# Two more split stages at the start of a fast-matrix-product kernel, earlier and smaller weight casts, and 2 KB pieces in DRAM

## The chip, the cores and the metric

The kernel runs on one core of a Trainium2 chip. The metric is the device time of one execution in microseconds (us). Three executions of the kernel before took 1366.88 to 1367.45 us, their median is 1367.18.

## The reference

`x` is 8192 rows (16 x 512) of 512 numbers. Each row has 8 router logits; a softmax makes 8 probabilities of them. There are 8 expert matrices of 512 x 2048. The output is the sum over the experts of probability times product:

```python
probs = softmax(router_logits)
for e in range(8):
    output += probs[:, :, e:e+1] * np.matmul(x, expert_weights[e])
```

Put otherwise, it is one product: a left matrix of 8192 rows and 8 x 512 columns (each row of x times each of its probabilities) times the stacked experts, 4096 rows and 2048 columns.

## The kernel before

**The recursion.** The big product isn't computed by the plain rule, but by a form of fast matrix multiplication in which a 2 x 2 block product takes 7 block products in place of 8, at the price of sums of blocks on both sides. This is done on two levels everywhere and on a third level in some places. The outer level makes products of the kinds r = 1 to 7 (code: `product(r, q)`, q = 0 to 15 names a pair of row blocks of 256). Product 1, called P1, multiplies the upper half of the experts (block B11, experts 0 to 3, columns 0 to 1023) and needs no sums of weights. The weights' blocks are B11, B12, B21 and B22, each in quarters (k, n) of 1024 x 512. Operands are float16, sums in PSUM are float32.

**Products, steps, stages, slots.** On the second level each product has seven steps in the order 1, 5, 6, 2, 7, 3, 4 (`STEPS`, L344), each of 8 matmuls with 512 columns, for output quarters of 128 x 512. Two products a and b make a stage. A stage has 14 slots, in which the steps take turns: slot 0 is step 1 of a, slot 1 step 1 of b, slot 2 step 5 of a, and so on (`run`, L875). Stages 0 to 5 hold P1 for q = 2, 3 and on to 12, 13. A step accumulates in one of three PSUM banks of its product, x (steps 1, 6, 7, 4), q (5, 3) and b (2). After a step, `post` (L551) copies or adds: in P1, steps 7 and 3 are an addition on VectorE (DVE) into an `h` tile ("accumulation" in what follows), the rest copies on ScalarE (ACT).

**Left operands.** For each product DVE makes `z` (t[0] and t[1], x times probability, 128x2048 float16), a difference `d` (s2, 128x1024) and "i" (z minus d). Step 1 and 5 need t[0], step 6 needs d, 2 and 4 need t[1], 7 and 3 need i. On the right, steps 5, 6, 7 and 4 need sums of weight quarters (`inner_sums`, L169), which are also made on DVE: "sum 5" to "sum 4", 128x4096 each.

**Split stages.** In a split stage (`third`, L823; `run_third`, L856) the steps 1 and 5 of both products, 32 matmuls, are themselves done by 7 products instead of 8. They are 14 parts, x1 to x7 (for step 1) and q1 to q7 (for step 5), of 4 matmuls with 256 columns each. They need four sums `s` of the two left operands (`Third.make`, L633) and four sums `t` of each of the two right operands (`Split.make`, L606), all 128x1024. After x5 and q5 ACT copies two halves of a bank (L661, L663); after x6, q6, x7 and q7 DVE adds (L666). So that PE doesn't wait for these, two pieces of other work are held back and put between the parts (`held`): the last two slots of the stage before (steps 4 of a and b). The order is x1 x5 q1 q5, held piece, x2 q2 x6 q6, held piece, x7 q7 x3 q3 x4 q4, then slots 4 to 13. Before the change P1's stages 2 to 5 are split (L1219), further stage 9 and six stages near the end.

**The order of DVE's work.** DVE executes in the order in which the code emits. The code keeps a queue of tasks (`later`, L370) and two clocks, "pe" and "dve" (L348). Each slot adds SLOT = 1.73 to pe; then, while dve is more than LAG = 0.3 behind pe, the next task is emitted and its cost added to dve (`slack`, L375; costs 1.14 for a z or i, 0.61 for d, s and t, 2.2 for a sum of weights). An accumulation is emitted after that, and adds 0.61 (`evacuated`, L381). A part of a split stage adds 0.44 to pe and emits no task; what it needs and what isn't there yet is emitted at once (`need`, L365). The left operands of stage k + 1 are queued at slot 1 of stage k (`queue_lefts`, L828): for a split stage both t[0], four `s`, both d, both t[1].

**Queues of transfers.** GpSimd (POOL) issues the stores of results and all casts of weights from float32 (`cast_w`, L145, 512 KB each), in the order of the code; SyncE (SP) issues loads of probabilities pT and x blocks, and transposes; ACT issues the fetches of kept weights and operands from DRAM (`fetch_w`, L164; `Operand.fetch`, L513). `at(stage, slot, ...)` (L698) puts something ahead of a slot. Weight tiles come from a pool of 15 buffers, `z` from 8, `h` from 13, x and pT from 9.

**Wedges.** From stage 4 to 9 (`wedge_at`, L982) a half of a quarter of B12 and of B22 is cast into one tile, 1024 KB in two casts, at slot 2; at slot 11 three DVE tasks are queued that make u = b - a, then two more sums in place, each stored to DRAM by POOL.

**The first phase** (L308 to L340) computes the plain product for the first rows (q = 0 and 1): it makes `z0` by small matmuls, then for two column halves n = 0, 1 runs e = 0 to 3 with 16 matmuls each, with the four results of a half copied by ACT (L337) and stored by SP. In between are the softmax and the first transposes `xT` and probabilities `pT` for stage 0. The end of the phase queues stage 0's work (L1234 to L1245).

Of the kernel before, what the change touches and what calls it, by code (L numbers as in the profile page):

```python
# [31 lines left out]
def kernel(  # L32
# [7 lines left out]
    nc = tc.nc  # L40
# [202 lines left out]
    def diag_e(e):  # L243
        return diag(ph0[0][:, e].unsqueeze(2))
# [15 lines left out]
    def early_xp1(j, d):  # L260
# [7 lines left out]
        evacuate(xp1[t][1][:, :, rows], ps.rearrange("p (e t) -> p e t", e=HE), 1)  # L268

    R = 4  # L270
    J = HQ // R
# [43 lines left out]
    for e in (1, 2):  # L315
        ds_.append(diag_e(e + 1))
        early_z0(e, ds_[e])
    for n in range(2):
        ps = [bank() for _ in range(4)]
        for e in range(HE):  # L320
            if n == 0 and e == 1:
                early_z0(3, ds_[3])
                ph0.append(early_p(1))
                ds_ = [diag_j(j) for j in range(4, 8)]
                keep_p = softmax_of_all()
                w, sums = inner_sums(b11, new_w())
# [8 lines left out]
        for j in range(4):  # L335
            o = half()
            act(nc.scalar.copy(o, ps[j]))  # L337
            sp(kept[j // 2][n].rearrange("(p j) m -> j p m", j=2)[j % 2], o)
        if n == 0:
            keep_p()  # L340

# [94 lines left out]
    class Left:  # L436
# [38 lines left out]
        def store(self, k):  # L475
            sp(self.kept[:, k], self.t[k])

# [29 lines left out]
    class Operand:  # L507
# [5 lines left out]
        def fetch(self):  # L513
            self.t = wpool.tile([P, 2, K8, HQ], f16, name="o", tag="w")
            note(nc.scalar.dma_start(out=self.t, in_=self.source))

# [75 lines left out]
    THIRD = (1, 5)  # L592
    COLS = [ds(i * HQ, HQ) for i in range(2)]

    class Split:
# [10 lines left out]
        def make(self, p, i):  # L606
            if i == 0:
                self.t[p] = wpool.tile([P, 4, C, HQ], f16, name="t", tag="w")
            w, t = self.right.op(p), self.t[p]
            block = lambda k, n: w[:, ds(k * C, C), COLS[n]]  # L610
            x, y = ((block(0, 1), block(0, 0)), (block(1, 1), t[:, 0]), (block(1, 1), block(0, 1)),
                    (block(1, 0), t[:, 1]))[i]
            tt(t[:, i], x, y, SUB)

        def op(self, p, m):
            if m in (1, 2, 3):
                k, n = ((0, 0), (1, 0), (1, 1))[m - 1]
                return self.right.op(p)[:, ds(k * C, C), COLS[n]]
            i = {5: 0, 6: 1, 7: 2, 4: 3}[m]
            need(self.task[p, i])  # L620
            return self.t[p][:, i]
# [125 lines left out]
    def product(r, q, **how):  # L747
# [18 lines left out]
        elif r == 6:  # L766
# [188 lines left out]
    def wedge(kn, e):  # L955

        t = new_w()
        a, b = t[:, ds(0, C), :], t[:, ds(C, C), :]
        rows = ds(e * C, C)

        def casts():
            cast_w(12, kn, e, a)
            cast_w(22, kn, e, b)

        def send(what, u):
            pool(kept_w(what, kn)[:, rows, :], u)

# [14 lines left out]
    def wedge_at(stage, slot, kn, e, then):  # L982
        made = []

        def begin():
            casts, made_ = wedge(kn, e)
            casts()
            made.extend(made_)

        def go_on():  # L990
            for make in made:
                later(1.14, make)
        at(stage, slot, begin)
        at(*then, go_on)

    b21, t1, t2, t3 = {}, {}, {}, {}

    def cast21(kn):
        b21[kn] = cast_block(21, kn)

    for i, kn in enumerate(((0, 0), (0, 1), (1, 1), (1, 0))):
        at(i + 1, 2, lambda kn=kn: cast21(kn))

# [25 lines left out]
    def odd_t():  # L1029
# [5 lines left out]
        def make3():  # L1035
            tt(made[12], made[22], made[12], SUB)
            pool(kept_w("t3", ODD), made.pop(12))

# [6 lines left out]
    def odd_t4():  # L1045
        def make():
            tt(made[21], made[21], t2[ODD], SUB)
            pool(kept_w("t4", ODD), made.pop(21))
        later(2.2, make)
# [34 lines left out]

    def part_of(what, kn, chunks):
        return kept_w(what, kn)[:, chunks, :]

    last_part = [None]

    def by_parts(stage, slot, every, r, load, between, when):  # L1090

        for j in range(4):
# [8 lines left out]

            def go_on(b=b, chunks=chunks):
                for kn in b:
                    if kn != ODD:
                        between(b[kn], kn, chunks)

            def end(b=b, chunks=chunks):
                last_part[0] = sums_in_place(lambda p, o: pool(part_of((r, p), (0, 0), chunks), o), b, r, 0.61, r == 3)
            at(*slots_after(stage, slot, j * every), begin)
# [11 lines left out]
    def load_part(what):  # L1121
        def load(t, kn, j, chunks):
            pool(t, part_of(what, kn, chunks))
        return load
# [3 lines left out]

    def less_t2(t, kn, chunks):
        def make():  # L1130
            tt(t, t, t2[kn][:, chunks, :], SUB)
            pool(part_of("t4", kn, chunks), t)
        later(0.61, make)

    def keep_raw(t, kn, chunks):
        pool(part_of("b22", kn, chunks), t)

# [138 lines left out]
```

## Time and profile before

| | us |
|---|---|
| median of 3 executions | 1367.18 |
| profiled execution | 1367.07 |
| its span (first to last instruction) | 1365.1 |
| PE busy | 1359.9 |
| DVE busy | 1126.5 |
| POOL busy | 407.0 |
| ACT busy | 195.7 |

A row of a timeline has the start (us from the span's start), the duration, the engine, the line, the operation, output<-inputs, the shape and the number of instructions merged into it, and in brackets the idle time before it and who ended that. Where instructions follow closely, a duration of 0.69 overlaps the next, which starts 0.6 later. A row of waits has who waited for whom, the total, how often, and the longest. The row on landing gives the least, middle and largest time from a transfer's issue to its arrival. A row of a DMA queue has its packets, megabytes, and the share of 16 engines' span that its packets took; a row of DMA issues has the count, the size and the middle time to landing.

### The profile page before, as it was taken

Reading aid. Unit: us, or ns where it says so; the run is one execution under the profiler, and the core shown is the slowest. Engines: PE = TensorE matmul, PEld = TensorE weight load, DVE = VectorE, ACT = ScalarE, POOL = GpSimd, SP = SyncE. Lnnn points to the kernel's source line nnn. Section 1 sums busy time; section 2 is a strip of 40 time slices with the busy share of each in tenths; the row PEclk is TensorE's granted clock in tenths of the full one; section 3 lists DMA queues with packets and bytes.
Section 4 is the critical chain, followed back from the end, with each engine's and each line's share of the span. In section 5 each row is a group of like instructions: output and inputs, shape, how many; then the busy total and the mean of one; then the engine's idle time right before and its main releaser. Section 6 shows DMA issues by size and latency. Waiting matters only on the chain.

```text
span 1365.1 us, 18194 instructions
## 1 busy us (share of the span) xinstructions
PE 1359.9 (100%) x6657; PEld 648.7 (48%) x6657; DVE 1126.5 (83%) x1367; ACT 195.7 (14%) x362; POOL 407.0 (30%) x644
## 2 busy tenths in 40 slices
PE   9999999999999999999999999999999999999998
PEld 4455544544444444444444444444444444456554
DVE  5975787989789788788887888888889797998873
ACT  3232311100011111111111100000000000123221
POOL 3123333331223342333322122242332422223232
PEclk9999999999999999999999999999999999999999
DMA  9999999999898999999999978989898979999896
GB/s 195 242 218 228 253 242 323 310 300 383 257 304 268 311 350 274 293 279 292 328 258 331 344 247 221 216 240 203 232 252 220 252 203 292 302 217 245 196 206 119
DMA packets 193385, 356.41 MB, mean 261 GB/s; under 512 B 53136, under 2 KB 87184, under 8 KB 188176
## 3 DMA queue, kind: packets, MB, share of 16 engines
q0 software_dynamic: 88048, 183.02, 55.3%
q1 hardware_dynamic: 99488, 132.25, 31.9%
q10 hardware_dynamic: 5760, 39.99, 7.6%
q8 instruction: 52, 0.85, 0.2%
q14 instruction: 37, 0.30, 0.1%
HBM read 214.47 MB, written 167.97 MB: 280 GB/s over the span
## 4 chain that ended last, share of the span: by engine, by line
PE 99%; DMA 0%; DVE 0%; issue 0%; ACT 0%; POOLq 0%
PE ps L132 99%; DMA w<-in_x_dram 0%; DVE z L238 0%; DVE h L112 0%; ACT h L1213 0%; POOLq L1260 0%
## 5 line engine op out<-in xcount | busy, mean ns | idle before, releaser
L132 PE MATMUL ps<-w,z 128*128 128x512 f16 x5240 | 1125.7, 375 | 0.0
L132 PEld LDWEIGHTS <-z 128*128 128x128 f16 x5328 | 521.2, 98 | 598.4
L126 POOL DMA_DIRECT2D out_dram<-h x380 | 249.3, 662 | 736.5 <-ACT h L582 352.6
L112 DVE TENSOR_TENSOR h<-ps,h 128x512 f32<-128x512 f32 x415 | 284.6, 687 | 184.7 <-PE ps L132 166.7
L112 DVE TENSOR_TENSOR z<-xT,pT 128x2048 f16<-128x2048 f16 x216 | 261.9, 1217 | 0.0
L132 PE MATMUL ps<-w,d 128*128 128x512 f16 x880 | 199.1, 379 | 0.0
L132 PEld LDWEIGHTS <-d 128*128 128x128 f16 x880 | 86.1, 98 | 101.5
L112 DVE TENSOR_TENSOR z<-z,d 128x2048 f16<-128x2048 f16 x110 | 131.7, 1217 | 0.0
L582 ACT COPY h<-ps 128x512 f32<-128x512 f32 x64 | 37.5, 585 | 524.5 <-PE ps L132 521.1
L112 DVE TENSOR_TENSOR w<-w 128x1024 f16<-128x1024 f16 (+2 forms) x88 | 100.0, 1146 | 1.8 <-PE ps L132 1.0
L571 ACT COPY h<-ps 128x512 f32<-128x512 f32 x90 | 52.7, 585 | 293.5 <-PE ps L132 264.1
L112 DVE TENSOR_TENSOR ps<-ps,h 128x512 f32<-128x512 f32 (+1 forms) x110 | 64.0, 585 | 26.0 <-PE ps L132 25.7
L112 DVE TENSOR_TENSOR d<-z 128x1024 f16<-128x1024 f16 x110 | 74.6, 687 | 5.1 <-PE ps L132 3.6
L568 ACT COPY h<-ps 128x512 f32<-128x512 f32 x90 | 51.8, 589 | 132.4 <-PE ps L132 129.6
L126 POOL DMA_DIRECT2D kept<-h x56 | 30.8, 549 | 110.9 <-ACT h L571 78.0
L126 POOL DMA_DIRECT2D wd<-w x78 | 44.2, 592 | 35.0 <-DVE w L112 27.5
L126 POOL DMA_DIRECT2D w<-in_expert_weights_dram x65 | 48.6, 778 | 19.5 <-issue 13.8
L112 DVE TENSOR_TENSOR u<-xT,pT 128x2048 f16<-128x2048 f16 x38 | 46.2, 1217 | 0.0
L112 DVE TENSOR_TENSOR h<-h 128x512 f32<-128x512 f32 (+2 forms) x69 | 45.1, 675 | 0.1
L112 DVE TENSOR_TENSOR z<-z,u 128x2048 f16<-128x2048 f16 x34 | 41.3, 1216 | 0.1
L112 DVE TENSOR_TENSOR z<-z 128x2048 f16<-128x2048 f16 x32 | 39.1, 1222 | 0.7
L564 ACT COPY ps<-ps 128x512 f32<-128x512 f32 x45 | 25.6, 570 | 94.4 <-PE ps L132 87.2
(61 smaller groups left out, 291.9 us busy)
## 6 DMA issues: line engine op xcount, KB each, us to landing
out_dram<-h POOLq DMA_DIRECT2D x380, 256.0 KB, 6.8
pT<-p_dram SPq DMA_DIRECT2D x125, 256.0 KB, 6.3
h<-kept SPq DMA_DIRECT2D x116, 256.0 KB, 6.7
w<-wd ACTq DMA_DIRECT2D x25, 1024.0 KB, 9.0
xT<-x SPq DMA_DIRECT2D x76, 256.0 KB, 6.8
w<-in_expert_weights_dram POOLq DMA_DIRECT2D x35, 512.0 KB, 10.9
wd<-w POOLq DMA_DIRECT2D x64, 256.0 KB, 6.6
h<-out_dram SPq DMA_DIRECT2D x60, 256.0 KB, 5.4
```

Source lines behind the costliest of these rows:

```text
L112: dve(nc.vector.tensor_tensor(out=o, in0=a, in1=b, op=op))
L126: note(nc.gpsimd.dma_start(out=o, in_=i, **how))
L132: note(nc.tensor.matmul(ps, z, w, start=start, stop=stop, skip_group_check=True))
L564: act(nc.scalar.copy(self.banks["b"], x))
L568: act(nc.scalar.copy(o[tn], q if p == 5 else x))
L571: act(nc.scalar.copy(o[TN[p]], b if p == 2 else x))
L582: act(nc.scalar.copy(o[tn], b))
```

## The change

- P1's stages 0 and 1 are split as well. The eight `t` sums of P1 move from stage 1's queue into the first phase (one ahead of the loop, three in n = 0, e = 1; sum 5 and the other four in n = 1, e = 0).
- The held pieces of stage 0 are the last two quarters of the first phase's last group, 8 matmuls in two pieces of 4 (0.87 on the clock each), the second with the four result copies and stores.
- At the end of the first phase both t[0] and the four `s` of stage 0 are emitted at once; the dve clock is then set to 1.2. Sum 6 follows, then d, t[1], sum 7; sum 4 comes after the i's.
- B21's eight casts, two at slot 2 of the stages 1 to 4, come one at a time at slots 5 and 12 of the stages 0 to 3.
- A wedge's first cast comes at slot 3 instead of 2, its second at slot 7 instead of 2; its sums stay at slot 11.
- Kept weight blocks lie in DRAM as 4 chunks of 128 rows with 2 KB, kept operands in 4 blocks likewise; before, a fetch read 8 KB per partition in one run.

```diff
-            stored[what, kn] = dram.tile([P, K8, NB], f16, name="wd")
-        return stored[what, kn]
+            stored[what, kn] = dram.tile([C, P, 2, NB], f16, name="wd")
+        return stored[what, kn].rearrange("a p b n -> p a b n")
...
-        note(nc.scalar.dma_start(out=t, in_=stored[what, kn]))
+        note(nc.scalar.dma_start(out=by_twos(t), in_=kept_w(what, kn)))
...
+    def early_thirds(p, some=range(4)):
+        if p not in early_t:
+            early_t[p] = new_t()
+        for i in some:
+            third_weights(w[p], early_t[p], i)
...
+    def first_product(ps, n, e, c, j):
+        mm(ps[j], z0[j][:, e, c], b11[e // 2, n][:, e % 2 * C + c, :],
+           e + c == 0, e == HE - 1 and c == C - 1)
+
+    def first_results(ps, n):
+        for j in range(4):
+            o = half()
+            act(nc.scalar.copy(o, ps[j]))
+            sp(kept[j // 2][n].rearrange("(p j) m -> j p m", j=2)[j % 2], o)
...
+    w, sums = inner_sums(b11, new_w())
+    early_thirds(1, (0,))
     for n in range(2):
         ps = [bank() for _ in range(4)]
         for e in range(HE):
             if n == 0 and e == 1:
                 early_z0(3, ds_[3])
+                early_thirds(1, (1, 2, 3))
...
+            if n == 1 and e == 0:
+                sums[5]()
+                early_thirds(5, (0,))
             for c, j in ORDERS[n == 0 and e == 0]:
-                mm(ps[j], z0[j][:, e, c], b11[e // 2, n][:, e % 2 * C + c, :],
-                   e + c == 0, e == HE - 1 and c == C - 1)
+                if n == 0 or e < HE - 1 or c < 2:
+                    first_product(ps, n, e, c, j)
             if n == 1:
                 for j in ((4, 5), (6, 7), (), ())[e]:
                     early_xp1(j, ds_[j - 4])
-                if e == 1:
-                    sums[5]()
...
+                if e == 0:
+                    early_thirds(5, (1, 2, 3))
...
-    def slack():
+    def slack(slot=SLOT):
         clock["dve"] = max(clock["dve"], clock["pe"])
-        clock["pe"] += SLOT
+        clock["pe"] += slot
...
-                left.kept = dram.tile([P, 2, K8, HQ], f16, name=f"kept_left_{q}")
+                left.kept = dram.tile([2, 2, P, C, HQ], f16, name=f"kept_left_{q}")
...
         def begin():
             casts, made_ = wedge(kn, e)
-            casts()
-            made.extend(made_)
+            casts[0]()
+            made.extend(made_ + casts[1:])
 
         def go_on():
-            for make in made:
+            for make in made[:3]:
                 later(1.14, make)
         at(stage, slot, begin)
+        at(stage, slot + 4, lambda: made[3]())
         at(*then, go_on)
...
     for i, kn in enumerate(((0, 0), (0, 1), (1, 1), (1, 0))):
-        at(i + 1, 2, lambda kn=kn: cast21(kn))
+        for e in range(2):
+            at(*((i + 0,5), (i + 0,12))[e], lambda kn=kn, e=e: cast21(kn, e))
...
-        wedge_at(4 + i, 2, kn, e, (4 + i, 11))
+        wedge_at(4 + i, 3, kn, e, (4+i,11))
...
-    for stage in (2, 3, 4, 5):
+    for stage in (0,1,2,3,4,5):
         third(stage, 1)
-    at(1, 2, splits[1].queue)
+    splits[1].t = early_t
...
+    def last_first(c):
+        for j in range(4):
+            first_product(ps, 1, HE - 1, c, j)
+        if c == C - 1:
+            first_results(ps, 1)
+        slack(0.87)
+
+    for c in (2, 3):
+        held.append(lambda c=c: last_first(c))
     need_first = [right[1].task[p] for p in (6, 7, 4)]
     for p in (2, 3):
         lefts[1, p].queue_make(0)
+    thirds[0].queue_sums()
     queue.append(need_first[0])
+    flush(thirds[0].task[3])
+    clock["dve"] = 1.2
     for p in (2, 3):
         lefts[1, p].queue_s2()
     for p in (2, 3):
         lefts[1, p].queue_make(1)
-    queue.extend(need_first[1:])
+    queue.append(need_first[1])
+    at(0, 0, lambda: queue.append(need_first[2]))
```

More of the change, by code (lines that the diff above doesn't have):

```diff
@@ L268, in early_xp1, with third_weights, new_t @@
         evacuate(xp1[t][1][:, :, rows], ps.rearrange("p (e t) -> p e t", e=HE), 1)
+    COLS = [ds(i * HQ, HQ) for i in range(2)]
+    def third_weights(w, t, i):
+        block = lambda k, n: w[:, ds(k * C, C), COLS[n]]
+        x, y = ((block(0, 1), block(0, 0)), (block(1, 1), t[:, 0]), (block(1, 1), block(0, 1)),
+                (block(1, 0), t[:, 1]))[i]
+        tt(t[:, i], x, y, SUB)
+    def new_t():
+        return wpool.tile([P, 4, C, HQ], f16, name="t", tag="w")
+    early_t = {}
+    def early_thirds(p, some=range(4)):
[3 more added lines that the diff above has]
+            third_weights(w[p], early_t[p], i)
     R = 4
@@ L332 @@
                     early_xp1(j, ds_[j - 4])
-                if e == 1:
-                    sums[5]()
[L335 to L338, printed above, removed]
+                if e == 0:
+                    early_thirds(5, (1, 2, 3))
         if n == 0:
+            first_results(ps, n)
             keep_p()
@@ L475, in store @@
         def store(self, k):
-            sp(self.kept[:, k], self.t[k])
+            sp(self.kept[k].rearrange("g p c t -> p g c t"), self.t[k].rearrange("p (g c) t -> p g c t", g=2))
         def queue_make(self, k):
@@ L592 @@
     THIRD = (1, 5)
-    COLS = [ds(i * HQ, HQ) for i in range(2)]
     class Split:
@@ L607, in make @@
             if i == 0:
[L608 to L613, printed above, removed]
+                self.t[p] = new_t()
+            third_weights(self.right.op(p), self.t[p], i)
         def op(self, p, m):
@@ L619, in op @@
             i = {5: 0, 6: 1, 7: 2, 4: 3}[m]
-            need(self.task[p, i])
+            need(self.task.get((p, i)))
             return self.t[p][:, i]
@@ L958, in wedge @@
         a, b = t[:, ds(0, C), :], t[:, ds(C, C), :]
[L959 to L963, printed above, removed]
+        rows, twos = ds(e * C, C), ds(2 * e, 2)
+        casts = [lambda: cast_w(12, kn, e, a), lambda: cast_w(22, kn, e, b)]
         def send(what, u):
-            pool(kept_w(what, kn)[:, rows, :], u)
+            pool(kept_w(what, kn)[:, twos], by_twos(u))
         def t3():
@@ L1036, in make3 @@
             tt(made[12], made[22], made[12], SUB)
-            pool(kept_w("t3", ODD), made.pop(12))
+            pool(kept_w("t3", ODD), by_twos(made.pop(12)))
         def make2():
@@ L1047, in make @@
             tt(made[21], made[21], t2[ODD], SUB)
-            pool(kept_w("t4", ODD), made.pop(21))
+            pool(kept_w("t4", ODD), by_twos(made.pop(21)))
         later(2.2, make)
@@ L1083, in slots_after, with part_of @@
         return stage, slot
-    def part_of(what, kn, chunks):
-        return kept_w(what, kn)[:, chunks, :]
+    def part_of(what, kn, j):
+        return kept_w(what, kn)[:, j]
     last_part = [None]
@@ L1100, in begin, with go_on, end @@
                     load(b[kn], kn, j, chunks)
[L1102 removed]
+            def go_on(b=b, j=j, chunks=chunks):
                 for kn in b:
                     if kn != ODD:
[L1105 to L1108 removed]
+                        between(b[kn], kn, j, chunks)
+            def end(b=b, j=j):
+                last_part[0] = sums_in_place(lambda p, o: pool(part_of((r, p), (0, 0), j), o), b, r, 0.61, r == 3)
             at(*slots_after(stage, slot, j * every), begin)
@@ L1122, in load @@
         def load(t, kn, j, chunks):
-            pool(t, part_of(what, kn, chunks))
+            pool(t, part_of(what, kn, j))
         return load
```

20 lines of the change are left out of this document (12 added, 8 removed).

## The prediction, made before the changed kernel was run

> **What bounds the kernel now.** First the page: its first two parts, then the chain that ended last; then the list of PE's waits.
>
> ```profile
> span 1365.1 us, 18194 instructions
> PE 1359.9 (100%) x6657; PEld 648.7 (48%) x6657; DVE 1126.5 (83%) x1367; ACT 195.7 (14%) x362; POOL 407.0 (30%) x644
> ...
> PEclk9999999999999999999999999999999999999999
> ...
> PE ps L132 99%; DMA w<-in_x_dram 0%; DVE z L238 0%; DVE h L112 0%; ACT h L1213 0%; POOLq L1260 0%
> ```
> ```profile
> PE ps L132 <- DVE h L112: 0.3, 1, 0.3
> ```
>
> The tensor engine works from end to end at full clock, and after its start it waits for another engine once, for 0.3 us. So the time is the sum of the matmuls: a change gains only what it takes off PE, and loses whatever wait it gives PE. All other parts below are asked one question: does PE wait?
>
> **What a split stage is worth.** The first matmuls with `d` are step 6 of the first product, at the same place in stages 0, 1 and 2. From 0 to 1 lies no split, from 1 to 2 one (stage 2's).
>
> ```profile
> 47.38 3.62 PE L132 MATMUL ps<-w,d 128*128 128x512 f16 x16
> ...
> 71.56 3.62 PE L132 MATMUL ps<-w,d 128*128 128x512 f16 x16
> ```
> ```profile
> 94.94 3.62 PE L132 MATMUL ps<-w,d 128*128 128x512 f16 x16
> ```
>
> 71.56 - 47.38 = 24.18 and 94.94 - 71.56 = 23.38: one split takes **0.80 us** off PE. By parts: a part of 4 matmuls lasts 0.44 (133.00 to 133.44 further down), 14 of them 6.12; the four steps that they replace are 4 x 1.73 = 6.92 (a stage of 14 steps is 24.18). Two more stages split: **-1.60 us**.
>
> **The first phase on DVE.** Step 6 of stage 0 begins at 47.38, so the stage begins at 47.38 - 6.92 = 40.46; with 8 matmuls of the first phase (1.73) held back into it, it will begin at 38.73.
>
> ```profile
> 14.08 1.29 DVE L238 CAST z<-ps 128x512 f16<-128x512 f32 x2 [1.84 <-PE ps L132]
> ...
> 22.86 2.20 DVE L112 TENSOR_TENSOR h<-h 128x512 f32<-128x512 f32 x4
> ...
> 28.78 1.29 DVE L238 CAST xT<-ps 128x512 f16<-128x512 f32 x2 [3.72 <-PE ps L132]
> ...
> 34.44 2.29 DVE L112 TENSOR_TENSOR w<-w 128x4096 f16<-128x4096 f16 x1
> 36.65 2.35 DVE L112 TENSOR_TENSOR z<-xT,pT 128x2048 f16<-128x2048 f16 x2
> ...
> 67.35 0.69 DVE L112 TENSOR_TENSOR s<-z 128x1024 f16<-128x1024 f16 x1
> ```
>
> Added are eight `t` (a 128x1024 subtraction like `s`: 0.69, the next starts 0.6 later) and moved up is sum 5 (2.2 from start to start). One `t` fits into the 1.84 idle; three (1.85) push the softmax's end from 25.06 to 26.9, inside the 3.72 idle; sum 5 then ends at 29.1 and the next `t` at 29.8, so the first pair of `xT` is 1.0 late, for which nobody waits before 36; the last three `t` end at 32.9, before the second pair. From 34.4 DVE makes both `z` (to 36.65), four `s` (0.69 each at most, to 39.4) and sum 6 (41.6). Part x1 at 38.73 and x5 at 39.17 need the first `z` and the first `s` (37.4): 1.8 us to spare. Cost 0; uncovered it is what DVE is late beyond that.
>
> **The shorter held pieces.** The two held pieces of stage 0 last 0.87 each instead of 1.73. After x5 ACT makes two copies of half a bank, here in stage 9, where x5 ends at 252.28 (q1 follows it):
>
> ```profile
> 252.28 0.60 PE L132 MATMUL ps<-w,z 128*128 128x256 f16 x4
> ```
> ```profile
> 252.54 0.36 ACT L661 COPY ps<-ps 128x256 f32<-128x256 f32 x1 [7.25 <-PE ps L132]
> 252.81 0.38 ACT L663 COPY h<-ps 128x256 f32<-128x256 f32 x1
> ```
>
> They are done 0.9 after the part; x2 will come 1.74 after it (two parts and a piece of 0.87). x6 ends at 42.66, its DVE addition (0.43) at 43.35, x7 starts at 43.96. The four result copies follow the second piece:
>
> ```profile
> 40.03 2.05 ACT L337 COPY h<-ps 128x512 f32<-128x512 f32 x4 [5.62 <-PE ps L132]
> ```
>
> From 43.5 they run to 45.6; the copy that step 6 needs follows to 46.2, and step 6 starts at 46.6. Cost 0, with only 0.4 to spare; the other end is some 0.5.
>
> **The order on DVE in stage 0 is where it costs.** DVE runs in the written order, and that is settled by the kernel's two clocks (SLOT 1.73, LAG 0.3; costs 1.14, 0.61, 2.2). I check it on the kernel before: there, in stage 0, the clocks put the next stage's z and `d` into slot 8, behind them the first accumulation of step 7; the timeline has that order, with the idle time that the clocks leave:
>
> ```profile
> 51.27 1.22 DVE L112 TENSOR_TENSOR z<-xT,pT 128x2048 f16<-128x2048 f16 x1
> ...
> 52.52 0.69 DVE L112 TENSOR_TENSOR d<-z 128x1024 f16<-128x1024 f16 x1
> ...
> 56.29 0.69 DVE L112 TENSOR_TENSOR h<-ps,h 128x512 f32<-128x512 f32 x1 [3.07 <-PE ps L132]
> ```
>
> Now the changed stage 0. The clocks start at pe 0, dve 1.2. Four parts: pe 1.76; first piece: 2.63, sum 6 runs, dve 3.96; four parts and two additions: pe 4.39, dve 4.74; second piece: 5.26, a `d`, 5.35; six parts: pe 7.90. Slot 4: pe 9.63; d, z: dve 9.65. Slot 5: 11.36; z, sum 7: 12.99. Slot 6: 13.09, nothing. Slot 7: 14.82; both i: 15.37. Slot 8: 16.55; sum 4, then step 7's accumulation: 18.18. Slot 9: 18.28; 18.18 is not under 17.98, so nothing but the accumulation: 18.89. Slot 10: 20.01; stage 1's first z, accumulation: 20.64. Slot 11: 21.74; its second z and step 3's accumulation: 22.39. **None of stage 1's `s` has run** when stage 1's part x5 asks for the first, so it is written behind the last accumulation of stage 0. That accumulation waits for PE to end slot 11, which is when x1 starts. Its latencies, from stage 4, whose x1 starts two parts, 0.87, ahead of the first row here (q1):
>
> ```profile
> 133.00 0.60 PE L132 MATMUL ps<-w,z 128*128 128x256 f16 x4
> 133.44 0.60 PE L132 MATMUL ps<-t,s 128*128 128x256 f16 x4
> ```
> ```profile
> 132.39 0.69 DVE L112 TENSOR_TENSOR h<-ps,h 128x512 f32<-128x512 f32 x1 [1.04 <-PE ps L132]
> 132.99 2.35 DVE L112 TENSOR_TENSOR z<-z,d 128x2048 f16<-128x2048 f16 x2
> ```
> ```profile
> 8.55 0.69 DVE L112 TENSOR_TENSOR h<-ident,ph 128x512 f16<-128x512 f16 x1
> ...
> 9.30 1.07 PE L132 MATMUL ps<-h,w 128*128 128x128 f16 x16 [0.29 <-DVE h L112]
> ```
>
> x1 starts at 132.13; the accumulation 0.26 later, the next DVE instruction 0.60 after it, `s` lasts 0.69, and PE starts 0.06 after DVE (9.24 to 9.30): 1.61, of which x1 covers 0.44. PE waits **+1.17 us**. Queued behind x5 is all of PE. The other three `s` are due at x6 and later, 3.5 us on, and are done by then. From stage 1 the clocks have slack again (eight `t` have left it), so no other stage repeats this.
>
> **B21 and the wedge casts.** B21's casts move ahead and apart on POOL, behind stores that nobody waits for: 0. Each wedge's second cast goes from slot 2 to 7, while the subtraction that reads it stays at slot 11. Stage 4:
>
> ```profile
> 147.95 0.57 POOL L126 DMA_DIRECT2D kept<-h  x1 [6.08 <-ACT h L571]
> ```
> ```profile
> 154.88 1.23 DVE L112 TENSOR_TENSOR u<-w 128x2048 f16<-128x2048 f16 x1
> ...
> 156.62 2.48 DVE L112 TENSOR_TENSOR w<-w 128x2048 f16<-128x2048 f16 x2
> 160.56 0.87 DVE L112 TENSOR_TENSOR ps<-ps,h 128x256 f32<-128x256 f32 x2 [1.47 <-PE ps L132]
> ```
> ```profile
> 162.46 1.04 PE L132 MATMUL ps<-t,s 128*128 128x256 f16 x8
> ```
>
> The cast now follows that store, at 148.5. Landing takes L. DVE waits in `u` if L is over 6.4; behind it stand an accumulation, the two other sums and the addition between x6 and x7 (1.14 + 0.60 + 2.4 + 0.43, and 0.06 to PE): ready at 153.1 + L, and PE wants it at 162.46, so PE waits for **L - 9.35**. What L is, from the 20 casts between 60 and 270 us, and from the one of stage 4 that went out alone (137.24):
>
> ```profile
> DMA to landing us min/median/max: 6.0/9.7/17.3
> ```
> ```profile
> DMA to landing us min/median/max: 6.5/6.5/6.5
> ```
>
> Bounds 0 to 8.0 us, nothing below (PE waits for no cast today). Most of the 20 left as twins and shared the engines; the lone one is the nearest, so I take 0. Stages 5 to 8 only delay `u`; PE meets it again at the next split stage, 9.
>
> **Pieces of 2 KB.** Weights and operands fetched by ACT come in 2 KB instead of 8 KB runs.
>
> ```profile
> q0 software_dynamic: 88048, 183.02, 55.3%
> ...
> q10 hardware_dynamic: 5760, 39.99, 7.6%
> ```
> ```profile
> o<-kept_left ACTq DMA_DIRECT2D x13, 1024.0 KB, 11.1
> ```
> ```profile
> 1222.20 0.83 ACTq L515 DMA_DIRECT2D o<-kept_left  x2
> ```
> ```profile
> 1237.20 1.22 DVE L112 TENSOR_TENSOR z<-z,o 128x2048 f16<-128x2048 f16 x1
> ```
> ```profile
> 1252.66 0.60 PE L132 MATMUL ps<-t,s 128*128 128x256 f16 x4
> ```
>
> q10 moves 39.99 MB in 7.6% of 16 x 1365 us (24 KB per us and engine), q0 with its 2.1 KB packets 15. At worst a fetch takes 1.6 times as long: 17.7 for an operand. The operand issued at 1222.2 is first read at 1237.2, 15.0 later, and PE asks for what is made of it (x5) at 1252.7: DVE would wait 2.7 us with 15 in hand. At best nothing, as no PE wait ends on a transfer. I take 0; other end, a few us if ACT's queue blocks. The Trainium skill (DMA: Bandwidth & Descriptors, Specifications) gives 512 B as enough for line rate, by which 2 KB costs nothing and this rival falls away; the two queues' rates above speak against it, though they also differ in who shares them.
>
> SP's four result stores move behind two pT loads that wait for buffers; they only hold `h` tiles longer. 0.
>
> **Sum.** Profiled execution 1367.07 (span 1365.1 and 2.0 around it): -1.60 + 1.17 = -0.43, so 1366.6; the median of the three runs is 0.11 above, so **1366.7**.
>
> **Rivals.**
> - *No wait at x5.* The clocks missed running a z in slot 9 by 0.2; if the `s` come one slot earlier, all 1.60 stays: 1365.6. Against it: the order came out right on the kernel before. 0.10.
> - *The late wedge cast, slower than before.* 1366.7 + (L - 9.35): over 1367.18 from L = 9.9, at 17.3 it is 1374.6. For it the median 9.7, against it the lone 6.5. 0.22, of it 0.10 beyond L = 12.5 (1369.9). The Trainium skill (TensorE: Matmul & The Clock Gate, Part 1) says an idle window of about 3.4 us halves the clock until a busy one has passed; that would add an estimated 1.7 us to an L beyond 12.8, and no row here shows it.
> - *2 KB fetches slow the later phases*: 1 to 4 us, 1367.7 to 1370.7. 0.05.
> - *The split does not give its gain*, because half-length held pieces leave x2, x7 or step 6 waiting (0.4 us spare): about 1367.2. 0.05.
> - The forecast: 0.58.
>
> 0.2% of 1367.18 is 2.73 us (1364.45 to 1369.91), about what a measurement of this kernel can tell from no change. Faster than that no case gives: 0.02. Slower: 0.10 from the cast, 0.03 from the rest. Within: 0.85. Range 1365.4 to 1369.6, from the first rival to the cast at L = 12.3.
>
> **What would show it.** In the profile after: PE's list of waits has a line with DVE `s`, 1.0 to 1.4 us, once, near 61 us; first `d` matmuls at about 46.6 and 71.2 instead of 47.38 and 71.56; no other PE wait. `u` waiting on a weight cast and PE idle near 161 or 257 would show the second rival. A PE wait on a transfer, or PE idle between 38 and 47, would make other steps wrong.

## The result and the profile after

The changed kernel takes 1375.28 us (median of 4 executions, 1373.35 to 1376.76), the kernel before beside it 1367.21 (1366.88 to 1367.45). The ratio is 1.0058 (95% interval 1.0046 to 1.0071): **8.1 us slower**. The forecast was 1366.7, the range ended at 1369.6.

The profiled execution of the changed kernel took 1373.35, the shortest of its four; its span is 1371.4, 6.3 more than before. The other three, 1.1 to 3.4 longer, show a mean granted clock of TensorE of 0.997 or 0.998 where this one shows 1.000; they have no timeline here, so what follows explains the 6.3 and not all of the 8.1. From the page's first part, and the list of PE's waits (total, how often, longest):

```profile
PE 1359.2 (99%) x6705; PEld 652.5 (48%) x6705; DVE 1132.9 (83%) x1383; ACT 198.0 (14%) x370; POOL 411.2 (30%) x644
```
```profile
PE ps L132 <- DVE h L112: 3.0, 3, 1.7
PE ps L132 <- DVE ps L112: 2.2, 3, 1.3
...
PE ps L132 <- DVE s L112: 1.0, 1, 1.0
PE ps L132 <- DMA w<-in_x_dram: 0.6, 1, 0.6
PE ps L132 <- DVE t L112: 0.3, 1, 0.3
```

PE has less to do (1359.2 for 1359.9), but now it waits, nearly always for DVE. Where, its timeline says:

```profile
46.47 3.62 PE L132 MATMUL ps<-w,d 128*128 128x512 f16 x16
...
61.90 0.61 PE L132 MATMUL ps<-t,s 128*128 128x256 f16 x4 [1.02 <-DVE s L112]
...
71.04 3.62 PE L132 MATMUL ps<-w,d 128*128 128x512 f16 x16
```
```profile
141.25 1.03 PE L132 MATMUL ps<-t,z 128*128 128x256 f16 x8 [0.55 <-DVE ps L112]
159.58 2.76 PE L132 MATMUL ps<-w,z 128*128 128x512 f16 x16 [1.74 <-DVE h L112]
165.25 1.03 PE L132 MATMUL ps<-t,s 128*128 128x256 f16 x8 [0.30 <-DVE ps L112]
256.26 0.60 PE L132 MATMUL ps<-t,s 128*128 128x256 f16 x4 [0.29 <-DVE t L112]
```
```profile
1212.07 2.76 PE L132 MATMUL ps<-w,z 128*128 128x512 f16 x16 [1.01 <-DVE h L112]
1218.74 1.03 PE L132 MATMUL ps<-t,s 128*128 128x256 f16 x8 [1.31 <-DVE ps L112]
```

How far each stage's step 6 (its first `d` matmul) starts from where it started before shows where the loss grows:

| first `d` of | before | after | difference |
|---|---|---|---|
| stage 0 | 47.38 | 46.47 | -0.91 |
| stage 1 | 71.56 | 71.04 | -0.52 |
| stage 3 | 118.32 | 118.03 | -0.29 |
| stage 4 | 141.70 | 142.12 | +0.42 |
| stage 5 | 165.08 | 167.91 | +2.83 |
| stage 7 | 213.42 | 216.26 | +2.84 |
| stage 9 | 260.98 | 264.66 | +3.68 |
| near the end | 1215.03 | 1221.41 | +6.38 |

Up to stage 3 all is near the forecast. Then come +0.7 and +2.4 in stages 4 and 5, +0.8 between the rows of stages 7 and 9, and +2.7 at 1212 to 1219; from stage 9 to 1195 us nothing is added. The rest of this document is about these three.

**Stages 4 and 5: a chain that begins in stage 1.** Each product's x and pT tiles are read by `z`, and a tile comes free when its last `z` is made. The blocks of x as loaded (`xs`, ahead of their transposes) are tiles of the same pool of nine (L434 of the changed kernel) and come free when their transposes have landed. First `z` on DVE, then the next stages' requests for x (`xs`, on POOL) and the transposes and pT loads on SP, before:

```profile
56.89 1.22 DVE L112 TENSOR_TENSOR z<-xT,pT 128x2048 f16<-128x2048 f16 x1
58.63 1.22 DVE L112 TENSOR_TENSOR z<-xT,pT 128x2048 f16<-128x2048 f16 x1
60.96 1.22 DVE L112 TENSOR_TENSOR z<-xT,pT 128x2048 f16<-128x2048 f16 x1
64.96 2.35 DVE L112 TENSOR_TENSOR z<-xT,pT 128x2048 f16<-128x2048 f16 x2
```
```profile
66.26 1.48 POOL L126 DMA_DIRECT2D xs<-in_x_dram  x2
```
```profile
59.42 3.10 SPq L123 DMA_DIRECT2D pT<-p_dram  x2
...
73.28 10.35 SPq L407 DMA_TRANSPOSE xT<-xs  x4
94.26 11.70 SPq L407 DMA_TRANSPOSE xT<-xs  x4
117.63 12.05 SPq L407 DMA_TRANSPOSE xT<-xs  x4
```

and after:

```profile
57.70 1.22 DVE L112 TENSOR_TENSOR z<-xT,pT 128x2048 f16<-128x2048 f16 x1
59.43 1.22 DVE L112 TENSOR_TENSOR z<-xT,pT 128x2048 f16<-128x2048 f16 x1
69.84 2.35 DVE L112 TENSOR_TENSOR z<-xT,pT 128x2048 f16<-128x2048 f16 x2
```
```profile
71.35 0.74 POOL L126 DMA_DIRECT2D xs<-in_x_dram  x1 [8.55 <-DVE z L112]
94.88 0.71 POOL L126 DMA_DIRECT2D xs<-in_x_dram  x1 [8.24 <-DMA xT<-xs]
...
119.87 1.45 POOL L126 DMA_DIRECT2D xs<-in_x_dram  x2 [9.85 <-DMA xT<-xs]
```
```profile
71.08 1.45 SPq L123 DMA_DIRECT2D pT<-p_dram  x2
```
```profile
73.54 19.53 SPq L441 DMA_TRANSPOSE xT<-xs  x4
101.95 16.10 SPq L441 DMA_TRANSPOSE xT<-xs  x4
126.18 17.10 SPq L441 DMA_TRANSPOSE xT<-xs  x4
```

In the unsplit stage 1 of before each product's t[1] follows its own t[0]: the `z` at 56.89 and 60.96 are t[1] (58.63 is b's t[0], and the pair at 64.96 belongs to stage 2). In a split one both t[1] stand behind the four `s` and both `d`: the two `z` before 69.84 are t[0], the pair at 69.84 is t[1]. With nine x/pT tiles, both requesters wait for that pair: POOL 8.55 us for x, SP till 71.08 for pT. The first group of transposes starts as before but takes 19.53 instead of 10.35, the second starts 7.7 later, the third 8.6. A group is two pairs, one for each block of x. SP's waits for landed transposes from 72 to 96 us, before and after:

```profile
SPq L407 <- DMA xT<-xs: 5.2, 1, 5.2
```
```profile
SPq L441 <- DMA xT<-xs: 12.1, 1, 12.1
```

So most of the longer time is SP standing still: it issues the second pair only when the first has landed, 6.5 to 7.3 us after issue before the change and 12.9 to 14.7 after. By the code, the second pair's tile can be the first block's `xs`, which is free only then; that it is so is inferred, and that this wait goes with a tenth tile (below) speaks for it. Why the first pair lands later isn't shown; the loads that had waited (71.08 to 72.5) go out just ahead of it. The whole slack of the transposes is gone, and DVE's `z` of stage 5 waits:

```profile
139.63 1.23 DVE L112 TENSOR_TENSOR z<-xT,pT 128x2048 f16<-128x2048 f16 x1 [1.86 <-DMA xT<-xs]
151.38 1.23 DVE L112 TENSOR_TENSOR z<-xT,pT 128x2048 f16<-128x2048 f16 x1 [9.86 <-issue]
```

Before, that second `z` ran at 140.49. "issue" means that the profile shows no releaser; in the splits-only run below the same `z` waits 12.86 for "DMA xT<-xs". Behind it in DVE's order stand all of the next stage's `s`, `d` and accumulations.

### The profile page after: what moved, and what is told of

It reads as the page before. It is cut to its first block, busy times and chain, and to the rows that moved or that the text cites. A ratio compares the mean times of both kernels' runs of the same rounds, so it can differ in the third digit from the quotient of the medians.

```text
span 1371.4 us, 18312 instructions
## 1 busy us (share of the span) xinstructions
PE 1359.2 (99%) x6705; PEld 652.5 (48%) x6705; DVE 1132.9 (83%) x1383; ACT 198.0 (14%) x370; POOL 411.2 (30%) x644
## 4 chain that ended last, share of the span: by engine, by line
PE 86%; DMA 7%; DVE 3%; issue 1%; POOL 1%; SPq 1%; ACT 0%; DVEq 0%; POOLq 0%
PE ps L132 86%; DMA xT<-xs 2%; DMA o<-kept_left 2%; DMA w<-in_expert_weights_dram 2%; DVE z L112 1%; DMA xs<-in_x_dram 1%; DMA kept<-h 1%; DVE h L112 1%; SPq L441 1%; DVE s L112 0%; DMA x<-xT 0%; POOL w L126 0%; DVE t L112 0%; DVE w L112 0%; DVE d L112 0%
## 5 line engine op out<-in xcount | busy, mean ns | idle before, releaser
L132 PE MATMUL ps<-w,z 128*128 128x512 f16 (+1 forms) x5208 | 1117.0, 374 | 2.9 <-DVE h L112 2.8
L126 POOL DMA_DIRECT2D wd<-w x78 | 47.0, 628 | 37.6 <-DVE w L112 26.8
L132 PEld LDWEIGHTS <-s 128*128 128x128 f16 x416 | 40.6, 98 | 11.2 <-issue 2.6
L132 PE MATMUL ps<-t,s 128*128 128x256 f16 x312 | 42.6, 273 | 2.9 <-DVE ps L112 1.6
## 6 DMA issues: line engine op xcount, KB each, us to landing
w<-wd ACTq DMA_DIRECT2D x25, 1024.0 KB, 13.4
```

Of the source, the lines that this page charges most:

```text
L126: note(nc.gpsimd.dma_start(out=o, in_=i, **how))
L132: note(nc.tensor.matmul(ps, z, w, start=start, stop=stop, skip_group_check=True))
```

## The experiments

The diff falls into parts that can be made alone: **splits** (all that makes stages 0 and 1 split), **wedge** (the wedge casts at slots 3 and 7), **B21** (its casts in halves), **pieces** (2 KB). All times are medians with the extremes; the kernel before, run beside them, has medians of 1366.99 to 1367.08. Where an interval includes 1, the difference isn't clear of the spread by itself.

| run | us | ratio to before |
|---|---|---|
| e1 splits only | 1372.32 (1370.78 to 1372.96) | 1.0034 [1.0021, 1.0048] |
| e2 pieces only | 1368.04 (1367.01 to 1368.83) | 1.0007 [0.9998, 1.0015] |
| e3 wedge and B21 only | 1368.68 (1366.73 to 1369.5) | 1.001 [1.0002, 1.0019] |
| e4 the whole change, 10 x/pT tiles | 1372.04 (1369.27 to 1374.19) | 1.0035 [1.0023, 1.0047] |
| e5 splits, 10 tiles | 1367.39 (1366.83 to 1372.68) | 1.0005 [0.9997, 1.0014] |
| e6 splits, 10 tiles, sum 4 moved | 1366.21 (1365.53 to 1367.24) | 0.9993 [0.9984, 1.0002] |
| e7 stage 0 split only | 1366.81 (1365.98 to 1367.63) | 0.9997 [0.9988, 1.0005] |
| e8 before, 10 tiles | 1368.33 (1367.36 to 1369.24) | 1.0007 [0.9998, 1.0015] |
| e9 splits, sum 4 moved, 9 tiles | 1370.72 (1365.37 to 1373.0) | 1.0019 [1.0008, 1.003] |
| e10 e6 and B21 | 1366.27 (1365.75 to 1367.09) | 0.9995 [0.9986, 1.0003] |
| e11 e6 and wedge | 1368.86 (1368.11 to 1371.17) | 1.0015 [1.0006, 1.0023] |
| e12 e6 and pieces | 1367.28 (1365.98 to 1371.61) | 1.0004 [0.9996, 1.0013] |
| e13 as e9, t[1] ahead of d in stage 1 | 1366.66 (1365.22 to 1368.26) | 0.9995 [0.9986, 1.0003] |
| e14 e6 and pieces of operands | 1366.66 (1366.03 to 1367.82) | 0.9998 [0.9989, 1.0006] |
| e15 e6 and pieces of weights | 1366.47 (1364.82 to 1373.54) | 0.9999 [0.9989, 1.0008] |

### Which part loses: e1, e2, e3

Each undoes the other parts of the diff. For e1 the 2 KB layout, the wedges and B21 go back, with all that belongs to them:

```diff
-            stored[what, kn] = dram.tile([C, P, 2, NB], f16, name="wd")
+            stored[what, kn] = dram.tile([P, K8, NB], f16, name="wd")
...
-        wedge_at(4 + i, 3, kn, e, (4+i,11))
+        wedge_at(4 + i, 2, kn, e, (4 + i, 11))
...
-            at(*((i + 0,5), (i + 0,12))[e], lambda kn=kn, e=e: cast21(kn, e))
+        at(i + 1, 2, lambda kn=kn: cast21(kn))
```

> Only the two split stages (with the early t sums, held pieces and s sums), casts and DRAM layout as before. Theory A (x buffers): splitting stage 1 keeps its x and pT tiles some 9 us longer, so POOL's xs loads and SP's transposes fall behind and the z of stage 5 comes late; then PE waits near 141 to 165 us for 2 to 3.5 us in all, plus 1.0 for s at 61.9, and the time is 1368 to 1370. Theory B (the moved casts crowd out the transposes): no wait near 141 to 165, only the 1.0 at 61.9, time 1366.6. In both no wait near 1212.

> Only the 2 KB pieces. Theory C (the fetch of an operand in 2 KB pieces lands up to 10 us later when it meets other traffic): PE waits 1.5 to 3 us near 1205 to 1216, time 1368.7 to 1370.2. Rival (those waits came from the shifted start of the phase, not from the pieces): no such wait, 1367.2.

> Only B21's casts in halves and sooner, and the wedge casts apart. Theory A: PE waits at most 0.3 to 1 us near 256 (a wedge's second cast lands behind its reader), time 1367.2 to 1368.2. Theory B: transposes late, PE waits 2 to 3.5 us near 141 to 165, time 1369 to 1371.

The splits alone lose 5.3, the casts 1.7, the pieces 1.05: 8.1 together, against the 8.1 of the whole. That it fits so well is partly luck, since the wedges alone cost 2.65 on another kernel below. The splits, the only part meant to take work off PE, lose most. PE's waits in e1, and the `z` that sets off the larger:

```profile
62.35 0.61 PE L132 MATMUL ps<-t,s 128*128 128x256 f16 x4 [1.02 <-DVE s L112]
161.59 4.45 PE L132 MATMUL ps<-w,z 128*128 128x512 f16 x16 [4.23 <-DVE h L112]
```
```profile
153.38 1.23 DVE L112 TENSOR_TENSOR z<-xT,pT 128x2048 f16<-128x2048 f16 x1 [12.86 <-DMA xT<-xs]
```

No cast is moved here, and the transposes are late all the same, so the moved casts aren't their cause. Beyond the wait at x5 all is lost in one place: step 6 of stage 4 starts 0.07 sooner than in the kernel before, that of stage 5 6.01 later, and so it stays to the end. In this execution the wait isn't all: the 16 matmuls behind it take 4.45, where the same 16 take 2.76 at 159.58 in the changed kernel, after an idle of only 1.74. The granted clock shows it (stretch, its length, PE's busy time and matmuls, granted clock, share and GB/s of the DMA engines):

```profile
157.00:161.60 4.60, 0.37 (x5) 1.00 1.18 318
161.60:165.00 3.40, 3.40 (x9) 0.51 1.08 348
165.00:167.00 2.00, 2.00 (x19) 0.98 1.05 412
```

The Trainium skill (TensorE: Matmul & The Clock Gate, Part 1), by which an idle window of about 3.4 us halves the clock, agrees. The 4.23 of idle cost another 1.69 here; in e9's profile (below) 4.25 of idle cost another 2.46, 5.22 for the same 16. The median of e1, above the 1370 at most that was expected, doesn't rest on this: three of its five executions show a clock of 1.000 and took 1370.78 to 1372.60. e3's waits are read further down, with e11, and e2's with e12.

### Buffers: e4, e5, e8

```diff
-    xpool = ctx.enter_context(tc.tile_pool(name="xpool", bufs=9))
-    hpool = ctx.enter_context(tc.tile_pool(name="hpool", bufs=13))
+    xpool = ctx.enter_context(tc.tile_pool(name="xpool", bufs=10))
+    hpool = ctx.enter_context(tc.tile_pool(name="hpool", bufs=12))
```

> The changed kernel with 10 buffers for x and pT tiles instead of 9, paid with 12 instead of 13 h buffers. Theory A: the xs load that waited from 62.8 to 71.3 goes out at about 62, and of the 3.3 us lost near 141 to 168 at least half come back: about 1.5 to 3 us under the changed kernel (1372 to 1374). Theory B: no change there, 1375. If 12 h buffers are too few, POOL or ACT wait for h and the time rises; the profile would show it.

> The two more split stages alone, with one x/pT buffer more (10 for 9) and one h buffer fewer (12 for 13). Theory A (the splits' whole loss is that stage 1's t[1] keeps x and pT buffers 9 us longer, so the transposes of stages 3 to 5 start late): the waits of stages 3 to 5 go, x5's 1.0 us stays, time is the one before - 1.60 + 1.02, about 1366.5. Rival D (the splits cost something that no buffer cures: crowded transposes, SP's order, DVE's order in stages 3 to 5): some of the +5.3 us remains, 1368 or more, and PE still waits for z or h between 140 and 170 us.

> The kernel before with 10 x/pT buffers and 12 h buffers, nothing else. Theory A: nothing waits for x buffers there, so the time is unchanged within 0.5 us. If it is faster or slower by more, the buffers' sizes matter by themselves, and the runs with 10 buffers are to be read against this one.

With a tenth tile the splits' loss goes from +5.3 to +0.3. POOL's request at 71.27 still waits for `z`, but that no longer reaches the next ones, and the groups of transposes are as short as before the change (e5; the next two take 10.88 and 9.97):

```profile
71.27 0.73 POOL L126 DMA_DIRECT2D xs<-in_x_dram  x1 [8.55 <-DVE z L112]
87.29 1.47 POOL L126 DMA_DIRECT2D xs<-in_x_dram  x2 [0.73 <-DMA w<-in_expert_weights_dram]
```
```profile
72.36 9.72 SPq L438 DMA_TRANSPOSE xT<-xs  x4
```

The first pair still lands late, in 9.5 to 12.5, but the second no longer stands behind it. Of PE's waits at x5 and in the stages 3 to 5 only x5's is left in e5, 1.02. e8 is needed to read this rightly: the tenth tile costs an `h` tile, and in the kernel before that alone is 1.25 slower (its interval just includes no change), since DVE waits 3.07 for an `h` that a store still holds, and PE for DVE:

```profile
1175.42 17.65 PE L132 MATMUL ps<-w,z 128*128 128x512 f16 x80 [1.18 <-DVE h L112]
```

Against e8, e5 is 0.94 faster; the two splits less x5's wait give 1.60 - 1.02 = 0.58. That is what e5's profile shows up to 1167 us, where step 6 starts 0.59 sooner than in the kernel before; 0.7 is lost from there to 1215. Three of e5's twelve executions took 1368.71 to 1372.68, and what happens in them no profile shows. e4, the whole change with 10 tiles, still loses 5.05: in its profile the waits of stages 4 and 5 are gone, and those of the wedges and the operands stay. Not all of it is in that one profile (its execution took 1369.37, the median is 1372.04).

### The wait at x5: e6

```diff
-    at(0, 0, lambda: queue.append(need_first[2]))
+    at(0, 2, lambda: queue.insert(list(queue).index(thirds[1].task[1]) + 1, need_first[2]))
```

> As the run with splits alone and 10 buffers, and sum 4 (2.2 us on DVE) is queued behind the first two sums s of stage 1 instead of ahead of its z. If the wait at x5 comes from sum 4 standing ahead, it goes: 1.0 us less than that run, about 1365.5, 1.6 under the kernel before. Rival: the wait moves (to slot 12, which needs sum 4, or to the later s), and the time is the same as that run's.

1.18 less than e5, and no wait near 62: the sum of 2.2 us in DVE's order, put ahead of stage 1's z, was the cause. e6 is 0.87 faster than the kernel before and 2.12 faster than e8, which has the same buffers; the interval of its ratio, 0.9984 to 1.0002, just includes no change. Expected was 1365.5. In its profile the whole gain is there up to 1167 us, step 6 at 1165.83 for 1167.47, which is 1.64; 0.6 of it is lost by 1215. e5, e10 and e14, also with 12 `h` tiles, lose 0.7 to 1.1 in that stretch, e13 with 13 nothing.

### One stage, and the place of t[1]: e7, e9, e13

e7 takes stage 1 out of the list of split stages. e9 is e6 with the old buffers. e13 adds to e9, in `queue_lefts`:

```diff
-                left.queue_s2()
+                left.queue_make(1) if stage == 1 else left.queue_s2()
             for left in two:
-                left.queue_make(1)
+                left.queue_s2() if stage == 1 else left.queue_make(1)
```

> Stage 0 split, stage 1 not; 9 buffers as in the kernel before. Theory A: stage 1's left operands are made in their old order, its z early, no buffer is held longer: 0.8 us under the kernel before, about 1366.2, no wait near 62 us and none at 140 to 170. If the first phase's new work (eight t, sum 5, held pieces) were part of the loss, it stays with this kernel: over 1367.

> The two more splits with sum 4 behind s0 and s1 of stage 1, but with the old 9 x/pT and 13 h buffers. With sum 4 moved, stage 1's t[1] is made some 1 to 3 us sooner than with the splits alone, so the x buffers come free that much sooner too. Theory A (9 buffers are too few once t[1] stands behind s and d): the transposes for stages 3 to 5 are still late and PE waits at 140 to 170 us, less than with the splits alone: 1367 to 1371. Rival: 9 buffers are enough once x5 isn't late; then 13 h buffers spare the wait near 1175 us as well and it is 1365.2 to 1366.0.

> The two more splits, sum 4 moved, old 9 x/pT and 13 h buffers, and in stage 1 alone both t[1] made ahead of both d instead of behind. Theory A says that the loss comes from how late t[1] frees the x/pT buffers: t[1] runs some 2 us sooner than with sum 4 moved alone (whose executions spread from 1365.4 to 1373.0), so the long executions should become fewer and the median fall under 1370.7; if 2 us is enough, all are at 1365.4 to 1366. Rival: it is not the time of t[1] but the traffic in the transfers: the spread stays as it is, median about 1370.7.

e7 gains 0.27, not 0.8, and its interval includes no change; but its profiled execution has the start-up load of weights 1.3 us late, as other profiles here have one load or another late (e2's the load of x, 1.5), and has no wait near 62 or 140 to 170. So the first phase's new work costs nothing that shows.

e9 and e13 make the buffer theory finer. The first t[1] of stage 1 starts at 69.84 in the changed kernel, 66.76 in e9 and 63.53 in e13; when it is made, POOL sends its second request, at 71.35, 68.28 and 65.05. From e9 to e13 the median goes from 1370.72 to 1366.66, with PE's work the same and only that order changed. (From e1, 1372.32, to e9 the wait at x5 goes too, 1.02 of the 1.60.) So the place of t[1] is a cause. But the first group of transposes in e9 and e13 still takes 18.74 and 20.17, with 12.0 and 12.3 of SP's waiting in it, and profiles of both still show the wait at stage 5, 4.25 and 2.33:

```profile
160.44 5.22 PE L132 MATMUL ps<-w,z 128*128 128x512 f16 x16 [4.25 <-DVE h L112]
```
```profile
157.93 2.76 PE L132 MATMUL ps<-w,z 128*128 128x512 f16 x16 [2.33 <-DVE h L112]
```

The second is e13's, whose profiled execution was its longest; its shortest took 1365.22. With nine tiles the splits stay at the edge; that the landing of the transposes decides each execution is likely, but the short ones have no profile.

### B21 and the wedges apart: e10, e11

> The splits with both cures (10 x/pT buffers, sum 4 moved: 1366.2) and the new B21 casts (in halves, one stage sooner, slots 5 and 12). If the B21 casts cost nothing on POOL and in the transfers: 1366.2 within 0.5. If the 1.7 us of both new casts together came from them, 1367.5 to 1368, with PE waits before 150 us.

> The splits with both cures (1366.2) and the new wedge casts (slots 3 and 7 for 2 and 2). Theory: the second cast, issued five slots later, lands too late for u in stages 7 and 8, and PE waits near 237 us (0.7) and 253 us (0.3): 1367.0 to 1367.5. Rival: those waits came from the B21 casts: then 1366.2 and none there.

Both edits are those of the change, put on e6. B21 costs 0.06: nothing. The wedges cost 2.65, more than the 0.8 to 1.3 expected:

```profile
237.15 3.62 PE L132 MATMUL ps<-w,d 128*128 128x512 f16 x16 [1.30 <-DVE ps L112]
252.73 0.60 PE L132 MATMUL ps<-t,s 128*128 128x256 f16 x4 [0.29 <-DVE t L112]
...
1175.44 17.65 PE L132 MATMUL ps<-w,z 128*128 128x512 f16 x80 [0.74 <-DVE h L112]
```
```profile
229.53 1.22 DVE L112 TENSOR_TENSOR u<-w 128x2048 f16<-128x2048 f16 x1 [5.04 <-DMA w<-in_expert_weights_dram]
```

Stage 7's `u` ran at 226.32 before and waited for nothing. Here it waits 5.04 for the late second cast, and everything behind it, i and the two additions, is late for PE at 237. In the changed kernel the cast itself stands in the chain:

```profile
223.07 9.86 DMA w<-in_expert_weights_dram
```

By the starts of step 6 the two waits cost 1.46 in stage 8 and 0.60 in stage 9, 2.06 of the 2.65. e3's profile has them too, 0.78 at 237.90 and 0.29 at 253.48, and e10's hasn't. The third, 0.74 at 1175, is a wait for an `h` as in e8. Twelve tiles alone don't make it: e3 with 13 has 0.47 there, and e6 with 12 has none so long. How late wedges bring it 900 us later isn't shown.

### The pieces: e12, e14, e15

> The splits with both cures (1366.2) and the 2 KB pieces for kept blocks and operands. Theory: operands fetched in 2 KB runs take up to 25 us near the end and PE waits for what is made of them near 1214 us: 0.8 to 2.7 more, 1367.0 to 1368.9. Rival: the piece size costs nothing (the 1.05 us of the pieces alone was the start-up load, 1.5 us late there): 1366.2 within 0.5.

> The splits with both cures (1366.2) and 2 KB pieces for the kept operands only; the kept weights as before. Theory: the operands' slow fetches near the end are what the pieces cost: PE waits near 1212 us, 0.5 to 1 us more, 1366.9 to 1367.3, with a few long executions of 1369 to 1371. Rival: 1366.2 and no long ones.

> The splits with both cures (1366.2) and 2 KB pieces for the kept weight blocks only; operands as before. Theory: weights are fetched stages ahead and cost nothing: 1366.2 within 0.4 and no long executions. Rival: their many packets crowd the other transfers (transposes, results), 1367 or more.

On e6 the pieces cost 1.07, of operands alone 0.45, of weights alone 0.26; the executions of e12 alone spread over 5.6. The times from issue to landing of the 25 fetches of weights by ACT, least, middle and largest, with weights in 8 KB runs (the kernel before):

```profile
DMA to landing us min/median/max: 5.0/9.0/13.8
```

and in 2 KB (the changed kernel; e15's middle is 13.2):

```profile
DMA to landing us min/median/max: 6.4/13.4/22.0
```

The weights' fetches are half as long again. The operands' middle time isn't longer in 2 KB (11.1 before, 10.0 after), but one of them, in the changed kernel, took 25.05 and DVE waited:

```profile
1178.67 25.05 DMA o<-kept_left
```
```profile
1203.82 1.22 DVE L112 TENSOR_TENSOR z<-z,o 128x2048 f16<-128x2048 f16 x1 [4.34 <-DMA o<-kept_left]
```

Before, that `z` ran at 1196.45. From it come the 1.01 and 1.31 at 1212 and 1219. So an operand's long fetch is what costs. Whether its own 2 KB runs or the weights' make it long can be read from five profiles, one execution each, by the last fetch of weights (1162 to 1168) and the pair of operands that ACT issues 10 us later:

| 2 KB runs | last weights landed in | slower operand of the pair | DVE waits for it | PE's wait near 1211 to 1219 |
|---|---|---|---|---|
| none (e6) | 8.7 | 12.5 | none | 0.16 |
| operands (e14) | 8.9 | 16.2 | none | 0.15 |
| weights (e15) | 20.0 | 18.2 | none | none |
| both (e12) | 17.1 | 23.3 | 3.30 | 0.79 |
| both (changed kernel) | 18.7 | 25.05 | 4.34 | 1.01 and 1.31 |

With weights in 2 KB runs their last fetch is still under way when the operands go out, and the operands land later; only both together make DVE wait for this pair. e2, both on the kernel before, has 23.4, 3.42 and 0.81. So the theory of e12 holds, and that of e14, by which the operands' own runs are enough, doesn't: the waits for other operands that e14 has (0.57 to 3.03) don't reach PE, and no execution of it is over 1367.82. e15's profile has a wait of its own, 1.14 for a `t` at 1182.62. The executions that reach 1371.61 and 1373.54 are of e12 and e15, with the weights in pieces; what happens in them no profile shows, and how the 1.07 is shared is within the spread.

## Why the prediction was wrong, point by point

- **The gain of a split: right.** Step 6 of stage 0 starts at 46.47 (46.6 was forecast), of stage 1 at 71.04 (71.2); with the waits cured, e6's profile has 1.64 up to 1167 us for a forecast of 1.60, and e6's median and the shortest executions of e9 and e13 are 0.9 to 1.8 under the kernel before.
- **The first phase, the held pieces, step 6: right**, no wait between 30 and 61.
- **The order on DVE in stage 0: right**, one wait for `s` at 61.90, 1.02 for a forecast of 1.17; e6 shows the cause.
- **"From stage 1 the clocks have slack again, so no other stage repeats this": the step that failed.** It asked only whether DVE has time for its tasks, not what the new order in stage 1 holds back. The kernel before shows t[1] at 56.89 and 60.96 and the two pT loads from 59.42; a split puts t[1] behind `s` and `d`, and the prediction had that order in hand, since it wrote stage 1's `s` ahead. It went through SP's queue only for the four result stores, and named pT loads "that wait for buffers" there without asking when those buffers come free. Nine tiles and the last reader's new time would have given a late x and pT; that the first pair of transposes then lands in 12.9 to 14.7 instead of 6.5 to 7.3, and SP stands 12.1 us before the second, had no row to be read from. Cost: some 5.9 of e1's loss (5.3 + 1.6 - 1.0). With t[1] back ahead (e13) or a tenth tile (e5) it goes for the most part.
- **The wedges: the mechanism was right, the size and the place wrong.** The landing L was taken at 6.5, the lone cast of stage 4, against a middle of 9.7; the cast that decided took 9.86. In stage 4 PE lost nothing (in e4 `u` waited 2.09 there). It was lost in stages 8 and 9: the prediction said that PE meets the delay only at the split stage 9, but i and the additions behind `u` made PE wait in stage 8, which isn't split. Measured: 0.8 in the changed profile, 2.06 in e11's, 2.65 in e11's median.
- **2 KB pieces: taken as 0, with the other end "a few us": the size was wrong.** The worst case had been put at 17.7 for an operand, 1.6 times the middle of 11.1; one took 25.05. The factor held (13.4 for 9.0 is 1.5, 25.05 for the longest before, 15.2, is 1.65); it had been put on the middle fetch, and one long fetch is enough for a wait. In the changed profile it is 2.3 of PE's waits, in the medians 1.05. The Trainium skill (DMA: Bandwidth & Descriptors, Specifications) gives 512 B as enough for line rate; the weights' 13.4 for 9.0 speak against reading that as "2 KB costs nothing" beside other traffic. The two rates of the queues, which the prediction weighed against it, were the better guide.
- **B21: right**, 0.06.

The rival on the clock gate was priced for the wedges alone, at 1.7 behind an idle of 3.4. It came at the transposes: 1.69 behind 4.23 in e1, 2.46 behind 4.25 in e9, so that the first equals the estimate is chance.

## What to carry to other kernels

When an edit moves a task later in an engine's order, look up which tiles it is the last to read, who asks for these tiles next, and how long that one's queue then stands; free time on the engine itself says nothing about it. In a program that is bound by one engine to 99%, a buffer pool that is exactly full is part of the schedule: one tile more was worth 5 us here, and one `h` tile less cost some 1.2. And where transfers vary, a change that leaves slack of 2 or 3 us on a transfer of 10 has to be priced at the middle or long landing, not at the shortest row at hand.

## What the runs showed of the hardware

After an idle of 4.23 us TensorE's next 16 matmuls took 4.45 instead of 2.76 us, and after 4.25 in e9 5.22, at a granted clock of 0.5; so a wait in this kernel costs more than its own length once it passes some point between 2.33 (no slowing, e13) and 4.23. A pair of DMA transposes landed 6.5 to 7.3 us after issue at 73 us in the kernel before and 9.5 to 16.1 at the same place in e1, e5, e9, e13 and the changed kernel; with nine tiles SP stood 11.3 to 12.3 us for that before it issued the next pair. And cutting DRAM runs from 8 to 2 KB made the middle 1 MB fetch by ACT 13.4 us instead of 9.0, while the share of queue q10's packets, weights and operands, rose only from 7.6% to 8.5%.
